# Batched matmul with both operands transposed: transposing b as bf16 pairs in 4-byte words, one batch ahead, with b loaded four rows to a partition

## The chip, the cores and the metric

The kernel runs on one core of one Trainium2 chip. The metric is the device time of one execution in microseconds (us); a profile's span, from the first to the last instruction, is about 1.7 us shorter than it. All inputs are random.

Names used below: PE is the TensorE, DVE the VectorE, ACT the ScalarE, SP the engine that issues all loads and stores. "The queue" is the one hardware queue of the 16 DMA engines; a DMA is served by all 16 and so lands in 16 parts. PSUM is the memory that PE writes its results to. The granted clock is the share of TensorE's full clock that the profile records.

## The reference

```python
# a: (16, 512, 512) f32 as (batch, k, m);  b: (16, 512, 512) f32 as (batch, n, k)
np.matmul(a.transpose(0, 2, 1), b.transpose(0, 2, 1)).astype(np.float32)
```

A batch loads 2 MB and stores 1 MB. `a` has k in rows, as the kernel's matmuls take it; `b` must be transposed on the chip.

## The kernel before

For each batch the kernel loads b and a (1 MB each, one DMA each), casts a to bf16 on ACT, transposes b in f32 on PE (16 transposes of 128x128), casts the result to bf16 on its way out of PSUM on DVE, does 16 matmuls of 128x128 by 128x512, and copies the four results out of PSUM, two on ACT and two on DVE. Stores are issued six batches late (LAG 6), so that loads have precedence and several stores stand behind the last load.

```python
    a_v = a.rearrange("b (ki ko) m -> b ki ko m", ko=KO)     # 4 rows of 2 KB side by side: 8 KB a partition
    b_v = b.rearrange("b (no ni) k -> b ni no k", ni=P)      # 4 separate rows of 2 KB a partition
    out_v = out.rearrange("b (mi mo) n -> b mi mo n", mo=MO)
    # ... pools: a_pool 3, b_pool 3, o_pool 8, psum_t 4, psum_o 4 ...
    LAG = 6
    # ...
    for i in range(B):
        b_sb = b_pool.tile([P, NO, K], f32)
        nc.sync.dma_start(b_sb, b_v[i])
        a_sb = a_pool.tile([P, KO, M], f32)
        nc.sync.dma_start(a_sb, a_v[i])
        # ... a_bf: four casts of 128x512 on ACT ...
        for rk in range(KO):
            bt_ps = psum_t.tile([P, N], f32)
            for no in range(NO):
                nc.tensor.transpose(bt_ps[:, no * P:(no + 1) * P], b_sr[:, no, rk, :], identity)
            nc.vector.tensor_copy(bt_sb[:, rk, :], bt_ps)
        # ...
        for rm in range(MO):
            o_ps = psum_o.tile([P, N], f32)
            for rk in range(KO):
                nc.tensor.matmul(o_ps, a_br[:, rk, rm, :], bt_sb[:, rk, :],
                                 start=(rk == 0), stop=(rk == KO - 1))
            if rm % 2 == 0:
                nc.scalar.copy(o_sb[:, rm, :], o_ps)
            else:
                nc.vector.tensor_copy(o_sb[:, rm, :], o_ps)
        if i >= LAG:
            emit_out_dma(i - LAG)
```

The source goes through a scheduler: it gives each engine its instructions.

## Time and profile before

129.46 us, median of 3 runs (129.3 to 129.65).

From the page of the kernel before: the span; then, in 40 equal slices, busy tenths of PE, the granted PE clock, the mean busy share of the DMA engines and what they moved; then the packets by size and the one queue's share of 16 engines' span.

```profile
span 127.8 us, 1405 instructions
...
PE   0099999999999995768767796877779777670000
...
PEclk9999999999999999999999999999999999998555
...
DMA  3999999999999999999999999999999999999980
...
GB/s 90 402 370 422 406 399 420 382 409 398 404 417 415 417 419 394 416 410 429 420 410 423 406 436 405 416 426 413 427 402 431 412 424 418 426 428 428 426 346 36
...
DMA packets 13063, 50.42 MB, mean 394 GB/s; under 512 B 768, under 2 KB 768, under 8 KB 8960
...
q1 hardware_dynamic: 13056, 50.33, 97.5%
```

The DMA row stands at 9 from the second slice to the thirty-eighth: in all this time the DMA engines are hardly ever idle. PE has slack from the sixteenth slice on. Of 13,063 packets 8,192 are the 2 KB packets of b (those under 8 KB less those under 2 KB).

The costliest groups on PE and DVE, with count, busy us and mean ns of one, then the idle time before them and its releaser:

```profile
L80 PE MATMUL o_ps<-bt_sb,a_bf 128*128 128x512 bf16 x248 | 59.0, 385 | 9.1 <-ACT a_bf L60 8.7
...
L73 DVE CAST bt_sb<-bt_ps 128x512 bf16<-128x512 f32 x64 | 40.0, 683 | 14.7 <-PE bt_ps L68 14.7
...
L68 PE MATMUL bt_ps<-identity,b_sb 128*128 128x128 f32 x256 | 35.7, 295 | 12.8 <-DMA b_sb<-in_b_dram 12.8
```

The trace has a record for each DMA packet and for each of the 16 parts of a DMA's landing. These give numbers that no view prints:

| | kernel before |
|---|---|
| 2 KB packet: typical duration; start to start on an engine | 84 ns; 80 ns |
| 8 KB packet: typical duration; start to start | 309 ns; 306 ns |
| one landing to the next, median part, load-only start | b 2.70 us, a 2.49 us |
| the same, stores at the end | 2.44 us |
| last landing of all (median part; last part) | 124.5 us; 127.0 us |

### The profile page before, as it was taken

Reading aid. Unit: us, or ns where it says so; the run is one execution under the profiler, and the core shown is the slowest. Engines: PE = TensorE matmul, PEld = TensorE weight load, DVE = VectorE, ACT = ScalarE, POOL = GpSimd, SP = SyncE. Lnnn points to the kernel's source line nnn. Section 1 sums busy time; section 2 is a strip of 40 time slices with the busy share of each in tenths; the row PEclk is TensorE's granted clock in tenths of the full one; section 3 lists DMA queues with packets and bytes.
Section 4 is the critical chain, followed back from the end, with each engine's and each line's share of the span. In section 5 each row is a group of like instructions: output and inputs, shape, how many; then the busy total and the mean of one; then the engine's idle time right before and its main releaser. Section 6 shows DMA issues by size and latency. Waiting matters only on the chain.

```text
span 127.8 us, 1405 instructions
## 1 busy us (share of the span) xinstructions
PE 92.5 (72%) x504; PEld 60.6 (47%) x512; DVE 61.5 (48%) x96; ACT 54.8 (43%) x97; POOL 0.7 (1%) x6
## 2 busy tenths in 40 slices
PE   0099999999999995768767796877779777670000
PEld 0094858678586763364634536353364634430000
DVE  0053668586774865463544727355472635640000
ACT  4026747646674635407163460816337072540000
POOL 2000000000000000000000000000000000000000
PEclk9999999999999999999999999999999999998555
DMA  3999999999999999999999999999999999999980
GB/s 90 402 370 422 406 399 420 382 409 398 404 417 415 417 419 394 416 410 429 420 410 423 406 436 405 416 426 413 427 402 431 412 424 418 426 428 428 426 346 36
DMA packets 13063, 50.42 MB, mean 394 GB/s; under 512 B 768, under 2 KB 768, under 8 KB 8960
## 3 DMA queue, kind: packets, MB, share of 16 engines
q1 hardware_dynamic: 13056, 50.33, 97.5%
q8 instruction: 4, 0.07, 0.2%
q14 instruction: 3, 0.02, 0.0%
HBM read 33.55 MB, written 16.78 MB: 394 GB/s over the span
## 4 chain that ended last, share of the span: by engine, by line
DMA 50%; PE 34%; SPq 3%; ACT 1%; issue 1%; DVE 1%; ACTq 0%
DMA a_sb<-in_a_dram 32%; PE o_ps L80 22%; DMA out_dram<-o_sb 13%; PE bt_ps L68 12%; DMA b_sb<-in_b_dram 4%; SPq L56 3%; ACT a_bf L60 1%; DVE o_sb L90 1%; ACT o_sb L88 0%; ACTq L60 0%; SPq L50 0%
## 5 line engine op out<-in xcount | busy, mean ns | idle before, releaser
L80 PE MATMUL o_ps<-bt_sb,a_bf 128*128 128x512 bf16 x248 | 59.0, 385 | 9.1 <-ACT a_bf L60 8.7
L60 ACT CAST a_bf<-a_sb 128x512 bf16<-128x512 f32 x64 | 34.9, 615 | 39.6 <-DMA a_sb<-in_a_dram 39.5
L73 DVE CAST bt_sb<-bt_ps 128x512 bf16<-128x512 f32 x64 | 40.0, 683 | 14.7 <-PE bt_ps L68 14.7
L68 PE MATMUL bt_ps<-identity,b_sb 128*128 128x128 f32 x256 | 35.7, 295 | 12.8 <-DMA b_sb<-in_b_dram 12.8
L80 PEld LDWEIGHTS <-a_bf 128*128 128x128 bf16 x256 | 27.3, 115 | 35.8 <-ACT a_bf L60 17.7
L68 PEld LDWEIGHTS bt_ps<-identity,b_sb 128*128 128x128 f32 x256 | 33.9, 211 | 17.5 <-PE o_ps L80 8.5
L90 DVE COPY o_sb<-o_ps 128x512 f32<-128x512 f32 x32 | 22.1, 692 | 38.9 <-PE o_ps L80 21.9
L88 ACT COPY o_sb<-o_ps 128x512 f32<-128x512 f32 x32 | 18.8, 586 | 19.0 <-PE o_ps L80 18.9
L60 ACT ACT_TABLE_LOAD x1 | 1.3, 1283 | 0.7 <-PEq L111 0.7
masks.py:199 POOL TENSOR_SCALAR_AFFINE_SELECT identity<-identity 128x128 f32<-128x128 f32 x1 | 0.3, 292 | 0.1
masks.py:197 POOL MEMSET identity<- 128x128 f32 x1 | 0.2, 204 | 0.3 <-POOLq L111 0.3
L111 POOL MEMSET const-bfloat16-1.0<- 128x1 bf16 x1 | 0.1, 101 | 0.0
L111 POOL MEMSET const-uint8-127<- 128x1 uint8 x1 | 0.1, 101 | 0.0
L111 POOL MEMSET const-float32-0.0<- 128x1 f32 x1 | 0.1, 98 | 0.2 <-issue 0.2
L111 POOL MEMSET const-float32-1.0<- 128x1 f32 x1 | 0.1, 98 | 0.0
## 6 DMA issues: line engine op xcount, KB each, us to landing
b_sb<-in_b_dram SPq DMA_DIRECT2D x16, 1024.0 KB, 15.4
a_sb<-in_a_dram SPq DMA_DIRECT2D x16, 1024.0 KB, 17.3
out_dram<-o_sb SPq DMA_DIRECT2D x16, 1024.0 KB, 17.4
```

The lines of the kernel that those rows point to most:

```text
L56: nc.sync.dma_start(a_sb, a_v[i])
L60: nc.scalar.copy(a_bf[:, rk, :], a_sb[:, rk, :])
L68: nc.tensor.transpose(bt_ps[:, no * P:(no + 1) * P], b_sr[:, no, rk, :], identity,)
L73: nc.vector.tensor_copy(bt_sb[:, rk, :], bt_ps)
L80: nc.tensor.matmul(o_ps, a_br[:, rk, rm, :], bt_sb[:, rk, :], start=(rk == 0), stop=(rk == KO - 1),)
L88: nc.scalar.copy(o_sb[:, rm, :], o_ps)
L90: nc.vector.tensor_copy(o_sb[:, rm, :], o_ps)
L111: nc = _bacc.Bacc("TRN2", target_bir_lowering=False, num_devices=1)
```

## The change

Loads: b comes with four neighbouring rows to a partition, 8 KB in one piece. Transposes: b is cast to bf16 first, two neighbouring bf16 values are taken as one 4-byte word, and the words are transposed, which halves the transposes to 8; since a partition now holds rows 4p to 4p+3, each transpose writes every fourth PSUM column, which puts n back in order; the matmul then reads every second bf16 value. Order: batch i+1 is to be cast and transposed ahead of the matmuls of batch i. Input buffers go from 3 to 4, output buffers from 8 to 6, those of the cast a from 4 to 3, LAG from 6 to 3.

```diff
--- before.py
+++ after.py
@@ -21,66 +21,75 @@
     B, K, M = a.shape
     _, N, _ = b.shape
     KO = K // P
+    KJ = KO // 2
     MO = M // P
     NO = N // P
 
     f32 = mybir.dt.float32
     cdt = mybir.dt.bfloat16
 
+
+
     a_v = a.rearrange("b (ki ko) m -> b ki ko m", ko=KO)
-    b_v = b.rearrange("b (no ni) k -> b ni no k", ni=P)
+    b_v = b.rearrange("b (ni no) k -> b ni no k", no=NO)
     out_v = out.rearrange("b (mi mo) n -> b mi mo n", mo=MO)
 
     const = ctx.enter_context(tc.tile_pool(name="const", bufs=1))
     identity = const.tile([P, P], f32)
     make_identity(nc, identity)
 
-    a_pool = ctx.enter_context(tc.tile_pool(name="a_pool", bufs=3))
-    b_pool = ctx.enter_context(tc.tile_pool(name="b_pool", bufs=3))
-    ac_pool = ctx.enter_context(tc.tile_pool(name="ac_pool", bufs=4))
+    a_pool = ctx.enter_context(tc.tile_pool(name="a_pool", bufs=4))
+    b_pool = ctx.enter_context(tc.tile_pool(name="b_pool", bufs=4))
+    ac_pool = ctx.enter_context(tc.tile_pool(name="ac_pool", bufs=3))
+    bc_pool = ctx.enter_context(tc.tile_pool(name="bc_pool", bufs=2))
     bt_pool = ctx.enter_context(tc.tile_pool(name="bt_pool", bufs=3))
-    o_pool = ctx.enter_context(tc.tile_pool(name="o_pool", bufs=8))
+    o_pool = ctx.enter_context(tc.tile_pool(name="o_pool", bufs=6))
     psum_t = ctx.enter_context(tc.tile_pool(name="psum_t", bufs=4, space=bass.MemoryType.PSUM))
     psum_o = ctx.enter_context(tc.tile_pool(name="psum_o", bufs=4, space=bass.MemoryType.PSUM))
 
-    LAG = 6
-    o_tiles = {}
+    LAG = 3
+    o_tiles, a_tiles, b_tiles, a_use, b_use = {}, {}, {}, {}, {}
 
-    def emit_out_dma(j):
-        nc.sync.dma_start(out_v[j], o_tiles.pop(j))
-
-    for i in range(B):
-        b_sb = b_pool.tile([P, NO, K], f32)
+    def load(i):
+        b_tiles[i] = b_sb = b_pool.tile([P, NO, K], f32, name="b_sb")
         nc.sync.dma_start(b_sb, b_v[i])
-        a_sb = a_pool.tile([P, KO, M], f32)
+        a_tiles[i] = a_sb = a_pool.tile([P, KO, M], f32, name="a_sb")
         nc.sync.dma_start(a_sb, a_v[i])
 
-        a_bf = ac_pool.tile([P, KO, M], cdt)
-        for rk in range(KO):
-            nc.scalar.copy(a_bf[:, rk, :], a_sb[:, rk, :])
-        a_br = a_bf.rearrange("p rk (pm rm) -> p rk rm pm", rm=MO)
+    def prepare(i):
+        b_sb, a_sb = b_tiles.pop(i), a_tiles.pop(i)
 
-        b_sr = b_sb.rearrange("p no (pk rk) -> p no rk pk", rk=KO)
-        bt_sb = bt_pool.tile([P, KO, N], cdt)
-        for rk in range(KO):
-            bt_ps = psum_t.tile([P, N], f32)
+
+
+        bc = bc_pool.tile([P, NO, K], cdt, name="bc")
+        nc.vector.tensor_copy(bc, b_sb)
+        bc_w = bc.bitcast(f32).rearrange("p no (pk j) -> p no j pk", j=KJ)
+        bt_sb = bt_pool.tile([P, KJ, N], f32, name="bt_sb")
+
+
+        for j in range(KJ):
+            bt_ps = psum_t.tile([P, N], f32, name="bt_ps")
+            bt_pw = bt_ps.rearrange("p (ni no) -> p no ni", no=NO)
             for no in range(NO):
-                nc.tensor.transpose(
-                    bt_ps[:, no * P:(no + 1) * P],
-                    b_sr[:, no, rk, :],
-                    identity,
-                )
-            nc.vector.tensor_copy(bt_sb[:, rk, :], bt_ps)
+                nc.tensor.transpose(bt_pw[:, no, :], bc_w[:, no, j, :], identity)
+            nc.vector.tensor_copy(bt_sb[:, j, :], bt_ps)
+        b_use[i] = bt_sb.bitcast(cdt).rearrange("p j (n h) -> p j h n", h=2)
 
-        o_sb = o_pool.tile([P, MO, N], f32)
-        o_tiles[i] = o_sb
+        a_bf = ac_pool.tile([P, KO, M], cdt, name="a_bf")
+        for h in range(2):
+            nc.scalar.copy(a_bf[:, 2 * h:2 * h + 2, :], a_sb[:, 2 * h:2 * h + 2, :])
+        a_use[i] = a_bf.rearrange("p rk (pm rm) -> p rk rm pm", rm=MO)
+
+    def multiply(i):
+        a_br, bt_h = a_use.pop(i), b_use.pop(i)
+        o_tiles[i] = o_sb = o_pool.tile([P, MO, N], f32, name="o_sb")
         for rm in range(MO):
-            o_ps = psum_o.tile([P, N], f32)
+            o_ps = psum_o.tile([P, N], f32, name="o_ps")
             for rk in range(KO):
                 nc.tensor.matmul(
                     o_ps,
                     a_br[:, rk, rm, :],
-                    bt_sb[:, rk, :],
+                    bt_h[:, rk // 2, rk % 2, :],
                     start=(rk == 0),
                     stop=(rk == KO - 1),
                 )
@@ -89,11 +98,18 @@
             else:
                 nc.vector.tensor_copy(o_sb[:, rm, :], o_ps)
 
-        if i >= LAG:
-            emit_out_dma(i - LAG)
 
+
+    for i in range(B + 1):
+        if i < B:
+            load(i)
+            prepare(i)
+        if i >= 1:
+            multiply(i - 1)
+        if i >= LAG + 1:
+            nc.sync.dma_start(out_v[i - 1 - LAG], o_tiles.pop(i - 1 - LAG))
     for j in range(B - LAG, B):
-        emit_out_dma(j)
+        nc.sync.dma_start(out_v[j], o_tiles.pop(j))
 
 
 # ---- launch: one core; inputs and outputs as the reference has them ----
```

## The prediction

> What bounds the kernel now: the DMA engines. The page's DMA row reads 9 in every slice from the second to the last but one; the hardware queue's packets fill 97.5% of 16 engines' span (124.6 of 127.8 us). PE is 72% busy, DVE 48%, ACT 43%; in the windows PE idles 3 to 5 us of every 20 after 40 us. The chain of waits has 34% PE, but also 32% landings of a_sb, for which PE waits. The last matmul ends at 114.4, the last store at 126.7. The Trainium skill, "DMA: Bandwidth & Descriptors", "Where 436 GB/s comes from", names a ceiling of 435 GB/s; the trace's 8 KB packets start every 306 ns on an engine, 428 GB/s for 16: no more bandwidth to win, only packet overhead.
>
> What the change does to that bound. Loads of b go from 8192 packets of 2 KB to 2048 of 8 KB (a and out have 8 KB already); bytes stay. A 2 KB packet takes 84 ns typically (86.2 mean) and starts every 80, so 8 KB of b cost 320 to 345 ns against 306 to 313. The landings agree: in the load-only start a b load takes 2.70 us of the queue, an a load 2.49, a store at the end 2.44. Gain: 16 x 0.15 to 0.21 = 2.4 to 3.4 us, on the engines that bound the span, thus on the critical path.
>
> Off that bound. PE: 256 f32 transposes become 128 (16 took 2.0 us, so 1 us less a batch), but write every fourth PSUM column. The skill's "SBUF — State Buffer", Door 1, says non-contiguous PSUM access slows matmuls; this trace has no such access. Even at double cost (0.26 us each) they take 2.1 us a batch, 16 matmuls 3.5; the sum stays under the DMA's 7.4 us a batch. The matmul's moving operand gets a 4-byte step; I expect it to keep its 0.22 us spacing. DVE: four casts of 0.68 become two f32 copies of about 0.69 and one 128x2048 cast, estimated 1.2 to 2.3 us: 4 to 5 us a batch with output copies. ACT: two casts of about 1.0 us for four of 0.615. None reaches 7.4. So transposes ahead of the previous batch's matmuls hide nothing that counts.
>
> Cost: LAG 3 leaves five stores after the last a load instead of seven. I estimate that out 14 and 15 are ready some 8 and 12 us after b 15 lands, with 10 to 12 us of queue left: a bubble of 0 to 1.5 us on the fast engines. Two engines lag by about 2.5 us at the end (last landing 127.0 against a median of 124.5), so most of it hides there; I charge 0.3 us.
>
> Predicted: 129.46 - 3.0 + 0.3 = about 126.7 us, 8 in 10 between 125.0 and 128.2. Chances: faster by over 2% 0.55, within 2% 0.43, slower 0.02.
>
> Right if: 6144 packets of 8 KB and none of 2 KB; b landings 2.45 to 2.5 us apart; the queue's time near 120 us; GB/s 415 to 428 from the third slice on; PE's share falls clearly; DMA row still 9 throughout.
>
> Wrong if: strided matmul reads or PSUM writes push PE past 7.4 us a batch (DMA row under 9); a hole in the DMA row in the last fifth (LAG 3, cold PE clock); the lagging engines, not packet size, set the end; or b's 8 KB reads stay slower than a's.

## More of the kernel before

Busy time by engine in stretches of the last 12 us (the last three columns are the granted clock, the DMA engines' share and their GB/s):

```profile
core 0: us, PE busy (x) PEld busy (x) DVE busy (x) ACT busy (x) POOL busy (x), PEclk, DMA share, GB/s
116.00:120.00 4.00, 0.00 (x0) 0.00 (x0) 0.00 (x0) 0.00 (x0) 0.00 (x0) 0.67 1.02 430
120.00:124.00 4.00, 0.00 (x0) 0.00 (x0) 0.00 (x0) 0.00 (x0) 0.00 (x0) 0.50 0.94 399
124.00:128.00 4.00, 0.00 (x0) 0.00 (x0) 0.00 (x0) 0.00 (x0) 0.00 (x0) 0.50 0.14 57
```

PE is done before the first of these stretches, and the queue runs full into the second: seven stores stand behind the last load, and the last one was issued at 115.2 us, long before its turn (the store ahead of it landed at 122 us).

## The result, and the profile after

127.98 us, median of 5 runs (127.54 to 130.0), against 129.3 us for the kernel before in the same rounds. The ratio is 0.9895, 95% interval 0.9866 to 0.9924. Here and below a ratio is the mean time of one kernel's runs over that of the other's of the same rounds, so not quite the ratio of the medians. Executions over 1.5% slower than the fastest of the same kernel are left out of the means. The gain is real but half of what was expected. The run whose profile was taken at first was a slow one (130.0 us), so the changed kernel was run again (after_again: 128.67 us, ratio 0.9908); its profile is used here. Medians in this document include slow runs: one of five here, one of four in after_again (128.94) and in source_order (128.26).

| | before | changed, run again |
|---|---|---|
| 2 KB and 8 KB packets | 8192 and 4096 | 0 and 6144 |
| b landing after the DMA ahead of it, load-only start | 2.70 us | 2.49 us |
| last part of the 47th of 48 DMAs landed | 124.6 us | 121.7 us |
| last part of the last DMA landed | 127.0 us | 126.0 us |
| issue of the last store | 115.2 us | 122.1 us |

The same lines of the changed kernel's page:

```profile
span 126.8 us, 1103 instructions
...
PE   0079979999948759578493948939578493993920
...
PEclk9999999999985995999999998699999999679998
...
DMA  3999999999999999999999999999999999999625
...
GB/s 119 419 434 414 434 432 416 414 289 429 416 434 414 424 437 421 424 434 424 424 437 419 424 432 416 421 439 416 424 437 421 421 434 421 426 419 426 277 111 230
...
DMA packets 6918, 50.41 MB, mean 398 GB/s; under 512 B 768, under 2 KB 768, under 8 KB 768
```

Read the DMA row from the right: it drops to 6 and 2 before the last store is written; GB/s falls to 277 and 111. And the granted PE clock, which was full to slice 36, now has four dips. The groups (L65 is the cast of b, L74 the transposes, L75 in the chain below the copy out of PSUM, L89 the matmuls, L99 the output copies on DVE):

```profile
L89 PE MATMUL o_ps<-bt_sb,a_bf 128*128 128x512 bf16 x249 | 67.8, 422 | 5.5 <-DVE bt_sb L75 3.0
...
L74 PE MATMUL bt_ps<-identity,bc 128*128 128x128 f32 x128 | 20.1, 304 | 29.1 <-DVE bc L65 29.1
...
L65 DVE CAST bc<-b_sb 128x2048 bf16<-128x2048 f32 x16 | 19.5, 1219 | 6.6 <-DMA b_sb<-in_b_dram 6.6
```

PE's matmuls are now costlier (422 against 385 ns in the mean, with the dips), the transposes are half as many at nearly the same price (304 against 295 ns). The last 12 us:

```profile
core 0: us, PE busy (x) PEld busy (x) DVE busy (x) ACT busy (x) POOL busy (x), PEclk, DMA share, GB/s
116.00:120.00 4.00, 3.66 (x19) 2.31 (x20) 1.46 (x3) 0.59 (x1) 0.00 (x0) 1.00 0.81 340
120.00:124.00 4.00, 1.33 (x6) 0.46 (x4) 1.21 (x2) 0.58 (x1) 0.00 (x0) 1.00 0.35 145
124.00:128.00 4.00, 0.00 (x0) 0.00 (x0) 0.00 (x0) 0.00 (x0) 0.00 (x0) 0.75 0.33 135
```

From 116 us on the DMA engines run at 81%, 35% and 33%, while PE still works on the last batch. So 2.9 us were won up to the 47th DMA (on the slowest engine; 2.2 on the median one), and 1.9 us given back at the 48th: on the slowest engine it landed 4.29 us after the one before it instead of 2.43, on the median engine 6.05.

Why is the last store late? The chain of waits (start us, length, what) of one batch in mid-run:

```profile
97.87 0.04 DVE o_sb L99
97.91 0.57 issue
98.48 1.23 DVE bc L65
99.71 0.14 issue
99.84 0.73 PE bt_ps L74 x4
...
100.60 0.70 DVE bt_sb L75
...
101.34 3.81 PE o_ps L89 x16
...
105.17 0.04 DVE o_sb L99
...
105.78 1.23 DVE bc L65
```

It is a closed loop over two engines: the last copy of the outputs on DVE, the cast of the next b on DVE (1.23), half of its transposes on PE (0.73), the copy out of PSUM on DVE (0.70), the 16 matmuls (3.81), the last copy again, and so on. (The 0.57 called issue is the rest of that copy, which takes 0.69.) From one cast to the next it takes 105.78 - 98.48 = 7.30 us. The DMA needs 7.37 us a batch (b 14 landed at 102.06 us, b 15 at 109.43). The loop thus has almost no slack, although no engine in it is 70% busy.

The intended order isn't there. In the source, PE gets T(0) T(1) M(0) T(2) M(1) and so on (T: 8 transposes, M: 16 matmuls of a batch). The order in which the compiled program issues them is:

```
changed:  T8 M9 T8 M21 T8 M17 T8 M16 T8 M17 T8 M16 T8 M16 ... T8 M16
```

After the first five batches T(i) stands directly before M(i), as in the kernel before. On DVE the cast of batch i+1 stands behind both output copies of batch i.

How late a batch is shows in one number: the start of the first instruction that reads b(i) less the landing of b(i), both from the trace.

```
lateness of b(i), us    i=5   6   7   8   9   10  11  12  13  14  15
before                  2.0 2.1 0.1 0.1 0.1 0.1 0.1 0.1 0.1 0.1 0.1
changed, run again      0.1 1.5 3.1 3.0 2.9 2.8 3.9 3.9 3.8 3.7 5.2
```

Before, from b 7 on, PE always waits for b. In the changed kernel b waits for the loop, and ever longer; each rise falls together with a dip of the clock (37.2, 47.5, 78.2 and 108.9 us, 3.4 us each; matmuls then start every 427 ns instead of 227). The dips start 10.3, 30.7 and 30.7 us apart: 3, 9 and 9 times their length of 3.41 us (in lag6 7 and 9 times, in evict_act 11 and 4). Each begins in, or up to 0.5 us after, a stretch of 3.5 us or more without an ordinary matmul, but there are eleven such stretches in this profile and four dips. How such a stretch lies against the steps of 3.41 us thus seems to decide; no run sets that position, so this is not shown.

### The profile page after: what moved, and what is told of

Its sections match the earlier page's. It is cut to its first block, busy times and chain, and to the rows that moved or that the text cites. A ratio compares the mean times of both kernels' runs of the same rounds, so it can differ in the third digit from the quotient of the medians.

```text
span 128.2 us, 1110 instructions
## 1 busy us (share of the span) xinstructions
PE 87.7 (68%) x384; PEld 46.2 (36%) x384; DVE 61.1 (48%) x80; ACT 50.7 (40%) x65; POOL 0.7 (1%) x6
## 4 chain that ended last, share of the span: by engine, by line
PE 49%; DMA 22%; DVE 16%; issue 7%; ACT 2%; SPq 1%; ACTq 0%
PE o_ps L89 42%; DMA a_sb<-in_a_dram 22%; DVE bc L65 10%; PE bt_ps L74 7%; DVE bt_sb L75 5%; ACT a_bf L80 2%; DVE o_sb L99 1%; SPq L55 1%; SPq L110 0%; ACTq L80 0%; SPq L57 0%
## 5 line engine op out<-in xcount | busy, mean ns | idle before, releaser
L89 PE MATMUL o_ps<-bt_sb,a_bf 128*128 128x512 bf16 x256 | 69.0, 424 | 5.2 <-DVE bt_sb L75 2.7
L89 PEld LDWEIGHTS <-a_bf 128*128 128x128 bf16 x256 | 30.0, 119 | 40.2 <-issue 15.6
L99 DVE COPY o_sb<-o_ps 128x512 f32<-128x512 f32 x32 | 22.1, 691 | 40.2 <-PE o_ps L89 21.5
L74 PE MATMUL bt_ps<-identity,bc 128*128 128x128 f32 x128 | 20.0, 302 | 29.9 <-DVE bc L65 29.9
L80 ACT CAST a_bf<-a_sb 128x1024 bf16<-128x1024 f32 x32 | 31.9, 1046 | 11.2 <-DMA a_sb<-in_a_dram 11.2
L74 PEld LDWEIGHTS bt_ps<-identity,bc 128*128 128x128 f32 x128 | 17.4, 209 | 35.8 <-issue 35.0
L75 DVE COPY bt_sb<-bt_ps 128x512 f32<-128x512 f32 x32 | 20.8, 687 | 14.6 <-PE bt_ps L74 14.6
L65 DVE CAST bc<-b_sb 128x2048 bf16<-128x2048 f32 x16 | 19.5, 1220 | 7.5 <-DMA b_sb<-in_b_dram 7.5
```

The lines of the kernel that those rows point to most:

```text
L65: nc.vector.tensor_copy(bc, b_sb)
L74: nc.tensor.transpose(bt_pw[:, no, :], bc_w[:, no, j, :], identity)
L75: nc.vector.tensor_copy(bt_sb[:, j, :], bt_ps)
L80: nc.scalar.copy(a_bf[:, 2 * h:2 * h + 2, :], a_sb[:, 2 * h:2 * h + 2, :])
L89: nc.tensor.matmul(o_ps, a_br[:, rk, rm, :], bt_h[:, rk // 2, rk % 2, :], start=(rk == 0), stop=(rk == KO - 1),)
```

## The experiments

Theory A, as it stood at first: the packet gain arrives; the compute has become a serial loop of 7.30 us a batch; dips of the PE clock put it behind, and with five stores behind the last load instead of seven, the queue runs dry before the last store. Rivals: B, DMA engines that lag behind the others set the end; C, strided PSUM writes or strided reads slow PE; D and F, the clock has no part in it; E, the lost order is the cause; and that five stores are too few as such. Ten runs were made, all correct.

| run | median us | ratio to before (95%) | b 15 late | last store issued |
|---|---|---|---|---|
| after_again | 128.67 | 0.9908 (0.983 to 0.999) | 5.2 us | 122.1 us |
| lag6 | 126.09 | 0.9753 (0.972 to 0.978) | 3.4 us | 114.0 us |
| evict_act | 126.70 | 0.9795 (0.975 to 0.984) | 0.1 us | 119.0 us |
| rows4 | 126.21 | 0.9767 (0.974 to 0.980) | 0.1 us | 112.1 us |
| warm | 127.92 | 0.9875 (0.985 to 0.990) | 4.9 us | 121.6 us |
| warm_late | 126.33 | 0.9770 (0.975 to 0.979) | 0.7 us | 117.9 us |
| source_order | 126.91 | 0.9769 (0.972 to 0.982) | 0.1 us | 120.1 us |
| rows_old | 129.88 | 1.0040 (0.999 to 1.009) | 5.1 us | 124.4 us |
| act_lag6 | 126.34 | 0.9755 (0.974 to 0.977) | 0.1 us | 109.8 us |
| rows4_lag4 | 126.69 | 0.9800 (0.977 to 0.983) | 0.1 us | 117.5 us |

The lateness and the issue are of each run's profile. The intervals of evict_act, source_order and rows4_lag4 reach over 0.98, so whether these three are faster than before by a full 2% stays unclear.

### after_again: the changed kernel once more

No edit. 

> The changed kernel once more, for a profile of a fast run. Theory A (the packet gain arrives, but the compute of one batch has become one serial chain of about 7.3 us through VectorE: cast of b, transposes, copies, matmuls, copy of o, next cast; a drop of the TensorE clock makes it 8.9; it falls behind the DMA, and with LAG 3 the queue runs dry before the last store): 127.5 to 128.4 us, b landings 2.48 us apart, a hole of 2 to 5 us in the DMA row before the last store. Rival B (the end is set by the one or two DMA engines that lag): no hole on the lagging engines, packets on them to the end.

The profile shown above: hole of 1.9 us on the slowest engine and 3.6 us on the median one. Three of its four runs took 128.6 to 128.9 us, a bit over the foretold 128.4, one 126.9. The mean granted clock of the three is 0.943 to 0.945, of the one 0.952, so that it probably had fewer dips; its trace was not kept. B is refuted here: all 16 parts of the last store landed within 0.2 us of each other (125.8 to 126.0), so no engine was still behind when it was issued.

### rows4: the four rows to a partition alone, in the kernel before

```diff
-    b_v = b.rearrange("b (no ni) k -> b ni no k", ni=P)
+    b_v = b.rearrange("b (ni no) k -> b ni no k", no=NO)
...
+            bt_pw = bt_ps.rearrange("p (ni no) -> p no ni", no=NO)
             for no in range(NO):
-                nc.tensor.transpose(bt_ps[:, no * P:(no + 1) * P], ...)
+                nc.tensor.transpose(bt_pw[:, no, :], ...)
```

> The kernel before with one part of the change: b four rows to a partition, transposes writing every fourth PSUM column; f32 transposes, order, buffers and LAG 6 as before. A: the packet gain alone, with compute that keeps ahead: 125.0 to 126.3 us, no 2 KB packets, transposes still about 0.13 us apart. B: 128.5 us or more. C: transposes at twice the spacing, 0.26 us.

126.21 us, ratio 0.9767: more than the whole change gave. The page of rows4:

```profile
DMA  3999999999999999999999999999999999999980
...
GB/s 89 428 425 423 439 423 420 420 418 420 423 383 412 418 423 418 425 433 425 425 415 423 439 428 415 433 420 420 436 428 423 431 420 418 431 425 433 425 370 39
...
DMA packets 6919, 50.42 MB, mean 404 GB/s; under 512 B 768, under 2 KB 768, under 8 KB 768
...
L69 PE MATMUL bt_ps<-identity,b_sb 128*128 128x128 f32 x256 | 35.7, 295 | 10.5 <-DMA b_sb<-in_b_dram 10.4
```

No 2 KB packets, no hole, and L69, the transposes that now write every fourth PSUM column, at the same 295 ns as L68 before (start to start 121 ns in both). The PSUM half of rival C falls. The other half, strided reads, has no run of its own: matmuls start every 227 ns in the changed kernel and 216 here, 0.18 us a batch that are part of the 7.30 us.

### rows_old: everything but that

```diff
-    b_v = b.rearrange("b (ni no) k -> b ni no k", no=NO)
+    b_v = b.rearrange("b (no ni) k -> b ni no k", ni=P)
...
-            bt_pw = bt_ps.rearrange("p (ni no) -> p no ni", no=NO)
+            bt_pw = bt_ps.rearrange("p (no ni) -> p no ni", no=NO)
```

> The changed kernel with b loaded as before (2 KB packets) and transposes writing contiguous PSUM columns: all of the change but the four rows to a partition. A: the DMA needs 7.5 to 7.6 us a batch again, and the end adds what is left of the hole: 129.0 to 130.5 us, no faster than the kernel before. Transposes as far apart as with strided writes (0.13 us); if contiguous writes make them faster, rival C has a part.

129.88 us, ratio 1.004: the rest of the change, with its halved transposes and its hole, is worth nothing in sum. The page of rows_old:

```profile
DMA  2999999999999999999999999999999999999725
...
DMA packets 13062, 50.41 MB, mean 390 GB/s; under 512 B 768, under 2 KB 768, under 8 KB 8960
...
L74 PE MATMUL bt_ps<-identity,bc 128*128 128x128 f32 x128 | 19.9, 301 | 30.6 <-DVE bc L65 30.6
```

The 2 KB packets are back and the hole is there as well. Transposes into contiguous columns start every 120 ns, as those with strided writes do in the changed kernel (120).

### lag6: more stores behind the last load

```diff
-    o_pool = ctx.enter_context(tc.tile_pool(name="o_pool", bufs=6))
+    o_pool = ctx.enter_context(tc.tile_pool(name="o_pool", bufs=10))
-    LAG = 3
+    LAG = 6
```

> The changed kernel with LAG 6 and ten output buffers; the compute is untouched. A: loads run three batches further ahead of the stores, so the chain starts its full-speed stretch about 6 us earlier, and eight stores instead of five stand behind the last load: the hole at the end closes, 124.3 to 125.8 us. B: as the change, 127.5 to 128.4 us.

126.09 us, 0.3 us over A's range and far from B's. The page of lag6:

```profile
PEclk9999999999999999958999999599999999859955
...
DMA  4999999999999999999999999999999999999981
```

The hole is gone although the loop and the dips are still there, and b 15 is 3.4 us late: its loads came 8 us earlier (b 15 landed at 101.5 us instead of 109.4), so the last store is issued at 114.0 us. Here the reserve in the queue made 3.4 us of lateness harmless.

### evict_act: the loop cut, LAG 3 kept

```diff
-            if rm % 2 == 0:
-                nc.scalar.copy(o_sb[:, rm, :], o_ps)
-            else:
-                nc.vector.tensor_copy(o_sb[:, rm, :], o_ps)
+            nc.scalar.copy(o_sb[:, rm, :], o_ps)
```

> The changed kernel with all four output copies of a batch on ScalarE (0.59 us each), none on VectorE, LAG 3 kept: the next cast of b no longer queues behind copies that wait for matmuls. A: a batch costs PE about 5 us, the DMA sets the pace again, the queue is never dry: 124.3 to 125.8 us. B, or a rival C (strided PSUM writes or strided matmul reads slow PE itself): 127 us or more.

126.7 us, better than the change by 1.1% in ratio (the two intervals just overlap), but 0.9 us over the range that A gave. The page of evict_act:

```profile
PEclk9999999999999999999869999999999869995996
...
DMA  4999999999999999999999999999999999999981
...
L65 DVE CAST bc<-b_sb 128x2048 bf16<-128x2048 f32 x16 | 19.6, 1226 | 49.1 <-DMA b_sb<-in_b_dram 49.1
```

DVE's casts now wait 49.1 us for loads of b: the loop is open, and each b but the fifth is taken up 0.1 us after it lands, although the clock dips at 61.5 and 99.1 us. What is left is one dip from 112.7 us on, under the very last batch (16 matmuls in 5.2 us), which puts the last store at 119.0 us and leaves a small hole (0.5 us on the median engine, none on the slowest).

### warm: PE kept busy, a miss

```diff
-    psum_t = ... bufs=4 ...
+    psum_t = ... bufs=3 ...
+    psum_w = ... bufs=1 ...;  warm_ps = psum_w.tile([P, N], f32)
...  at the end of multiply(i):
+        for _ in range(8):
+            nc.tensor.matmul(warm_ps, a_br[:, 0, 0, :], bt_h[:, 0, 0, :], start=True, stop=True)
```

> The changed kernel with eight more matmuls a batch, whose result nobody reads, in the 2 us in which PE waits for the next cast of b (one PSUM buffer of the transposes is given up for them); LAG 3 and the serial chain stay. Theory A says that the chain (7.30 us a batch against 7.37 of the DMA) has no slack, so that each 3.4 us of halved TensorE clock puts it behind for good, and the sum of these is the hole at the end. A: granted clock about 1.0 until the end, each batch's 16 matmuls 3.8 us, hole under 1 us, 125.8 to 126.8 us. Rival D (the chain's own length, or LAG 3, makes the hole, not the clock): 127.3 us or more.

127.92 us: D's number, not A's. The page of warm:

```profile
PEclk9999999999999999999999999999999999999999
...
DMA  4999999999999999999999999999999999999725
```

The clock was full and the hole stayed. The lateness tells why: 5.6 us at b 5, then 5.6, 5.5, 5.4 ... down to 4.9 at b 15. The eight extra matmuls had also stood in the way of the first five batches, where b lands every 5 us, and the loop, at 7.30 us a batch, made up less than 0.1 us a batch afterwards. So A had to be widened after the fact: what counts is that lateness, from any source, is hardly recovered (0.7 us in ten batches). The dips are one source.

### warm_late: the same from batch 5 on

```diff
-        for _ in range(8):
+        for _ in range(8 if 5 <= i < B - 1 else 0):
```

> As warm, but with the eight idle matmuls only in batches 5 to 14, so that they don't hold up the first batches (in warm the cast of b 5 was 5.6 us late, and the chain of 7.30 us never made it up). Theory A in its present form: lateness once incurred stays, from whatever source; here only the clock windows before batch 5 are left, so the cast of b 15 is 0.5 to 2.5 us late instead of 5.2, the last store is issued near 118 us instead of 122, the hole is under 1 us: 125.9 to 126.9 us. Rival F (the clock plays no part, the chain is late for another reason): 127.3 us or more again, b 15 over 4 us late.

126.33 us, ratio 0.977. The page of warm_late:

```profile
PEclk9999999999986999999999999999999999999995
...
DMA  3999999999999999999999999999999999999980
```

One dip, before batch 5; b 15 is 0.7 us late, the last store issued at 117.9 us, and no hole. With 80 useless matmuls added, the mean is 1.6 us below that of after_again (126.45 against 128.08; 1.4% in ratio). F falls: in the changed kernel it is the dips that make the loop late.

### source_order: the order that the source asks for

```diff
+    ctx.enter_context(tc.manual_schedule())    # every engine issues in the order of the source
     for i in range(B + 1):
```

> The changed kernel with every engine made to issue in the order of the source, so that the transposes of batch i+1 do stand ahead of the matmuls of batch i, which in the compiled order they don't from the fifth batch on. If the lost order were the cause (rival E), this restores the intended gain: 125.5 to 126.3 us. A says that it does not help: the cast of b still stands behind the copies of o on VectorE, the cycle becomes about 6.85 us, and at the end the matmuls of batch 14 now wait for b 15 as well, so that two batches of matmuls (7.6 us) follow the last b: 126.5 to 127.8 us, with a hole before the last store.

126.91 us in the median, but 128.3 in a slow one; the ratio is 0.9769. The median is A's, the ratio's interval reaches into E's range, so this run alone doesn't tell them apart. A's "does not help" was wrong in any case: against 0.9908 of the changed kernel the ratio is 1.4% better, and the two intervals don't overlap. PE's timeline in mid-run:

```profile
96.47 1.19 PE L74 MATMUL bt_ps<-identity,bc 128*128 128x128 f32 x8 [2.01 <-DVE bc L65]
97.50 3.80 PE L89 MATMUL o_ps<-bt_sb,a_bf 128*128 128x512 bf16 x16
103.49 1.20 PE L74 MATMUL bt_ps<-identity,bc 128*128 128x128 f32 x8 [2.19 <-DVE bc L65]
104.52 3.80 PE L89 MATMUL o_ps<-bt_sb,a_bf 128*128 128x512 bf16 x16
```

The matmuls now follow the transposes of the next batch, but the transposes still wait 2 us for the cast, as A said: on DVE the cast stands behind the output copies in the source's order too. The loop is 6.85 us in the middle of the run (casts at 47.2, 54.1, 60.9, 67.7 us), so it makes up 0.5 us a batch: b 5 is 6.5 us late, b 14 0.1 us. The clock row of the page has no dip until PE is done:

```profile
PEclk9999999999999999999999999999999999999997
```

The mean granted clock of its four runs was 0.983 to 0.994, against 0.943 to 0.952 in after_again, and the stretch without an ordinary matmul is 3.04 us in mid-run instead of 3.51. A small hole stays before the last two stores, since M(14) waits for b 15. The lost order was thus worth 0.45 us a batch of slack, and with it restored the dips were gone too, although PE still waits 2 us for each cast: E holds in part.

### act_lag6: both cures

The edits of evict_act and lag6 together. 

> The two cures together: all output copies on ScalarE and LAG 6 with ten output buffers. A: each alone took the hole away, the DMA bounds both, so together they add nothing over the better one: 125.5 to 126.2 us, last landing near 123.5 us, set by the one or two DMA engines that lag. If it is faster than 125.3, something other than the DMA was still limiting the others.

126.34 us, 0.1 us over A's range, ratio 0.9755 against 0.9753 of lag6: nothing is added, and it is not below 125.3. The DMA row reads 9 from the second slice to the thirty-eighth, and the last landing came at 123.7 us, as in lag6 (123.5). The DMA sets the time in all of these.

### rows4_lag4: are five stores too few?

```diff
 (rows4)
-    a_pool, b_pool: bufs=3;  o_pool: bufs=8;  LAG = 6
+    a_pool, b_pool: bufs=4;  o_pool: bufs=6;  LAG = 4
```

In this kernel's loop, LAG 4 gives the same order of loads and stores as LAG 3 in the changed one.

> rows4 with the changed kernel's order of loads and stores and its buffers (out of batch i-4 behind the loads of batch i, six output and four input buffers), so that five stores stand behind the last load as in the change, but with the compute of before. A: five stores are enough when the compute is not late; transposes of b 15 within 0.3 us of its landing, no hole: 126.0 to 126.7 us. If the small reserve of stores were a cause by itself: 127.3 us or more, with a hole.

126.69 us, ratio 0.980. The page of rows4_lag4:

```profile
DMA  4999999999999999999999999999999999999981
...
GB/s 107 424 429 424 432 424 418 421 306 424 416 418 426 426 432 403 418 429 421 426 426 424 426 426 429 413 432 426 426 426 426 432 424 426 424 421 429 432 356 50
```

No hole, b 15 0.1 us late. Five stores are enough when the compute is on time. Its ratio is 0.3% above that of rows4, within the intervals; the GB/s row has a dip in the ninth slice (306), in the load just ahead of the first store, which is taken up below.

## Why the prediction was right or wrong

**The number: inside the stated range, and in part by luck.** 127.98 us lies within 125.0 to 128.2, near its upper end, but the middle of the range, 126.7, was missed by 1.3 us, the outcome called likeliest (faster by over 2%, 0.55) did not come, and the median when run again, 128.67, lies outside. Of the marks under "right if" the packets, the landings and the queue's time (95.4% of 126.8 us, 121.0) came true; GB/s and the DMA row did not, and PE's share fell only from 72 to 68%. One of the marks under "wrong if", a hole in the last fifth of the DMA row, did come true. A right packet gain and a missed hole added up to a time that the wide range still held.

**The bound: right.** The DMA engines bounded the kernel before, and b's packet size was what the change could win. rows4 shows it alone (0.9767), rows_old shows that all the rest won nothing in sum (1.004). (In the DMA row the last slice but one is 8, not 9 as the prediction has it.)

**The size of the packet gain: right.** Predicted 3.0 us; 2.9 us at the 47th DMA on the slowest engine, 2.2 on the median one; in rows4, without the rest of the change, 3.1 and 2.9. b's landings came 2.49 us apart, as predicted (2.45 to 2.5). The upper end of the estimate, 3.4, is the difference of the landings (0.21 us a load); the mean durations of packets, which the prediction also lists, would have given 16 x 8 x 0.032 = 4.1.

**The skill's ceiling: agrees.** "DMA: Bandwidth & Descriptors", section "Where 436 GB/s comes from", has 435 GB/s; 8 KB packets that start every 306 ns are 428 GB/s, and the DMA rows of rows4 and lag6 move 408 to 439 in nearly all full slices (a slice counts a packet by its start, so a single one can read a little high).

**Costs of the single operations: right.** The cast of b took 1.22 us and DVE 4.0 us a batch (4 to 5), a's cast 1.05 (1.0), and transposes started every 120 ns. The matmul's operand with a 4-byte step was expected to keep its 0.22 us: it went from 216 to 227 ns, a twentieth.

**The step that failed: "None reaches 7.4. So transposes ahead of the previous batch's matmuls hide nothing that counts."** It compared the busy time of each engine by itself with the DMA's time. In the trace the engines take turns: a loop through DVE and PE takes 7.30 us a batch, though PE is busy for about 5 of them and DVE for 4. With that loop, being late is hardly made up (0.07 us a batch), and the dips of the clock, which the prediction named only under what would make it wrong, made it late. In the compiled order the cast stands behind both output copies from the fifth batch on, and the transposes directly before their own matmuls; the text took the order from the change's intent. Either part undone eased the loop: with the copies off DVE the casts wait for b alone (evict_act), in the source's order the loop is 6.85 us (source_order).

**The term of the sum that was mis-sized: "I charge 0.3 us" for the bubble.** It measured 1.9 us on the slowest engine, 3.6 on the median one. The queue that is left when b 15 lands was sized right: 109.4 us to the landing of store 14 at 119.8 (median part) or 121.7 (last part), 10.4 to 12.3 us. The last store's readiness, "some 12 us", looks right too (issued 12.7 us after b 15), but that is luck: its 8 us for out 14 suggest that it put M(14) between T(15) and M(15). In the compiled order it takes 7.5 us from the cast of b 15 to the issue (warm_late: b 15 at 109.6, 0.7 us late, issue at 117.9), and 5.2 us are lateness. From the issue to the first packet of the last store pass another 0.8 us (122.12 to 122.95), which the text left out. It also left out that, with LAG 3, the load just ahead of the first store took 3.5 us instead of 2.5 (median part, a 4; the last section has more of it). And "most of it hides there", in the lag of two engines, held in part only: the slowest is 1.8 us behind the median (121.67 against 119.83), so of 3.6 us it hides 1.8.

The sum with measured terms: 129.3 - 2.9 + 1.9 = 128.3 us, where 127.98 and, run again, 128.67 were measured. The prediction without its 0.3 us for the hole, 126.5, is close to what lag6, rows4, warm_late and act_lag6 measured (126.1 to 126.3).

The best kernels are lag6, act_lag6, rows4 and warm_late, equal within their intervals, 2.3 to 2.5% faster than before. rows4 is the simplest: three lines.

## What to carry to other kernels

Before costing a change by engine, close the loop: follow one batch through the engines in the compiled order of instructions and add up the times from a cast to the next cast. A loop as long as the DMA's time for a batch is a second bound, even at 70% busy, and it hardly makes up a delay. If the DMA is the bound, keep enough stores behind the last load to cover the latest that the last batch can be.

## What the Trainium skill lacked or had wrong

- "TensorE: Matmul & The Clock Gate", "HAM oscillation — how this bites in real kernels", gives the rule of no idle gaps of PE over about 3.4 us. Here the clock halved, for 3.4 us at a time, with PE gaps of 2.0 and 0.3 us around 8 transposes, a stretch of 3.5 us without an ordinary matmul. Filling the 2.0 us with matmuls removed the dips (warm_late: none from 39.7 us until PE is done). In rows4 stretches of 3.7 us, with 16 transposes in them, had none; rows4_lag4 had one dip, after a stretch of 5.4 us. The section itself doesn't say how transposes count; here neither the single gaps nor the stretch without ordinary matmuls tells by itself. PE was busy 39 to 48% of the 3.41 us before each of the four dips, but also 45 to 47% in three stretches of that length without a dip, so that no threshold comes out.
- "SBUF — State Buffer", "Door 1: The DMA port swizzle", says that "any non-contiguous PSUM access pattern significantly slows down matmuls". For transposes no run shows it: those that write every fourth f32 column start every 121 ns, those with contiguous columns too (rows4 and before; 120 and 120 in the changed kernel and rows_old). A bf16 moving operand with a step of two elements, which the same note counts as free, came with 227 ns a matmul against 216; that the step is the cause is argued, not shown.
- "Runtime: NRT & Kernel Launch", "Instruction fetch mechanics", calls the cost of a 16 KiB block mostly hidden. In this DMA-bound kernel it doesn't seem hidden: each such packet (the page's queue of kind instruction, 16,384 B, 3 or 4 in a run) took about 1.0 us (0.88 to 1.10). In the kernel before the first came at 27.0 us, and the last part of the landings fell from 0.75 to 2.0 us behind the median at the next DMA (27.27 against 26.52, then 31.00 against 29.01). In the other profiles too the lag grew by 0.6 to 1.6 us within 3 us of the first such packet; that the packet is the cause is argued from this. In the end the last engine is 2.5 us behind the median.
- No page has this: in the load just ahead of the first store, 8 KB packets mostly took 0.4 to 0.7 us instead of 0.31 (changed kernel, 25.3 to 27.8 us), and the ninth slice fell to 289 to 362 GB/s in the kernels with five stores in reserve and 8 KB loads. With LAG 6 the first store comes later and the dip is small (lag6 408, act_lag6 400, rows4 383 at worst). No run here explains it.
